# Attention: some of VectorE's subtractions are tied behind others

## The chip, the cores and the metric

The kernel runs on one core of one Trainium2 chip. The number that counts is the time of one execution on the device, in microseconds (us); smaller is better. All matrix products run in float32r, so that a float32 operand is cut into a high part (a rounded copy) and a low part (the operand less its high part), and a product takes three matmuls: high by high, high by low, low by high. The names in the profile follow this: `w_hi`, `w_lo` for weights, `h_hi`, `h_lo` for the normalised input, `wh`, `wl` for the attention weights.

## The reference

One block of a hybrid decoder: attention and an RWKV-7 time mix side by side, then an MLP and gated embeddings. The change lies in the attention and in the projections that run beside it.

```
def stick_breaking_attention(q, k, v):          # (B, S, H, Dh), 8 heads of 64, S = 512
    for blk in range(seq // Q_BLOCK):           # 128 queries each
        z = einsum('bhqd,bhkd->bhqk', q[block], k[:kend]) * scale
        mask = s_pos < t_pos
        log_om = where(mask, log_sigmoid(-z), 0.0)
        rev = cumsum(log_om, reverse=True)
        log_w = log_sigmoid(z) + rev - log_om
        w = where(mask, exp(log_w), 0.0)
        outs.append(einsum('bhqk,bhkd->bhqd', w, v[:kend]))

def reference(x, ...):
    h = rms_norm(x, attn_norm_g)
    u = h @ w_in                                # 1024 x 5376: q, k, v, time mix, gates
    o_sb = stick_breaking_attention(q, k, v)
    o_rw = rwkv7_time_mix(u_rw, ...)
    merged = g_sb * (o_sb @ w_up_sb) + g_rw * (o_rw @ w_up_rw)
    x = x + merged @ w_out
    ...                                         # MLP, embeddings, final norm
```

## The kernel before

**Weights.** Weights come in units of 128x1024 float32. `fetch_to` makes a unit ready: a DMA fills `w_raw`, ScalarE (ACT) casts it to `w_hi` (L225), and VectorE (DVE) subtracts to get `w_lo` (L227, 128x1024). It runs ahead of use: while one unit is multiplied, two further ones are fetched, and there are three buffers of `w_hi` and `w_lo`. In the attention stage the units are q, k and v of each pair of heads and then the first units of the time mix.

**Projections.** A projection of q, k or v is 8 steps of `mm3` (L244, L245, L246: three matmuls of 128x512 into `ps_m`, or `ps_z` for two of the early ones). `projected` then takes the result out of PSUM on DVE (L447 for q, L459 for k, L467 for v). For q it makes the high halves on ACT and GpSimd (POOL) and the low halves `ql` on DVE (L455, two of 64x512); for k the high halves `kk` on ACT (L462) and the low ones on DVE (L463, two of 64x512); v is turned by PE and split (L477, L478).

**Attention.** There are eight heads, in four pairs. `scores` makes three blocks of z in PSUM for a head (L511 with high q, L512 with low q, L513 for the mask), softplus of it on ACT (L516, L517, L518) and DVE (L519), and splits that into `sph` (ACT, L274) and `spl` (DVE, L275). Partial sums of it go through DVE (L528, L531) and POOL (L527, L532, L533). `attend` adds the running sums with PE (L558 and L562, from `sph`, `spl` and the sums), takes the exponential on ACT (L563), makes `wh` (L564) and `wl` (L565) on DVE, and multiplies them with v on PE (L550); L571 and L572 take the output out of PSUM.

**Order.** `drive` interleaves the steps of a head's `attend`, of the next head's `scores`, and 11 steps of the projections ahead. Each engine runs its own queue in order. The order within a queue is made when the program is built, by a scheduler that goes by dependencies and its own estimates of time; `tc.issue_after(x)` adds one more condition, that what is written inside it stands behind x in the queue of the same engine. `state["lo"]` is the last DVE subtraction of `split`, which is the helper for `sph` and `spl`.

Of the kernel before, what the change touches and what calls it, by code (L numbers as in the profile page):

```python
# [14 lines left out]
ALU = mybir.AluOpType  # L15
# [25 lines left out]
U_PLE, U_QKV, U_RW, U_GSB, U_GRW, U_UPSB, U_UPRW, U_OUT, U_FF1, U_FF2, U_GATE = range(11)  # L41
# [52 lines left out]
def tile_block(ctx: ExitStack, tc: tile.TileContext, xT, xt, pT, wts, lora, cols_d, gfin_d, consts_d, out, dbg=None):  # L94
    nc = tc.nc
    act, dve, pool, pe, sync = nc.scalar, nc.vector, nc.gpsimd, nc.tensor, nc.sync
# [3 lines left out]
    def r32(ap):  # L100
        return ap.bitcast(F32)
# [34 lines left out]
    seq = []  # L136
# [24 lines left out]
    state = {"i": 0, "used": 0, "due": 0}  # L161
    AHEAD = 3
    homes = {}
# [32 lines left out]
    def made(i):  # L196
# [10 lines left out]
            return sums12.pop(seq[i][1:])[:, 2]  # L207
        return loaded[i]

    def fetch_to(n, ahead=0):  # L210
        while state["i"] < min(n, len(seq)):
            i = state["i"]
            state["i"] += 1
            load_to(i + 1 + ahead)
            raw = made(i)
            if seq[i] in homes:
                hi, lo = homes[seq[i]]()
            elif seq[i][0] == U_S4:
                hi = wpool.tile([P, 512], F32R, name="w_hi4", bufs=1)
                lo = wpool.tile([P, 512], F32R, name="w_lo4", bufs=1)  # L220
            else:
                hi = wpool.tile([P, 1024], F32R, name="w_hi")
                lo = wpool.tile([P, 1024], F32R, name="w_lo")
            with tc.issue_after(state["hx"] if seq[i] == (U_FF1, 4) else state["fourth"][0]) if seq[i] in ((U_FF1, 4), (U_OUT, 2), (U_OUT, 3)) else nullcontext():
                state["cast"] = act.copy(out=hi, in_=raw).ins  # L225
            with tc.issue_after(state["fourth"][1]) if seq[i] in homes and seq[i][0] == U_OUT else nullcontext():
                state["wlo"] = dve.tensor_tensor(out=lo, in0=raw, in1=r32(hi), op=ALU.subtract).ins  # L227
            if seq[i] == (U_OUT, "s", 4):
                state["fourth"] = state["cast"], state["wlo"]
            ready.setdefault(seq[i], []).append((hi, lo))  # L230
# [42 lines left out]
    def split(hi, lo, src):  # L273
        act.copy(out=hi, in_=src)  # L274
        state["lo"] = dve.tensor_tensor(out=lo, in0=src, in1=r32(hi), op=ALU.subtract).ins  # L275
# [54 lines left out]
    with ExitStack() as sA:  # L330
# [43 lines left out]
        with ExitStack() as s1:  # L374
# [68 lines left out]
            def projected(hp, i, ps):  # L443

                if i == 0:
                    t = p1.tile([P, T], F32, name="qT", tag="qkv", bufs=3)
                    dve.scalar_tensor_tensor(out=t, in0=ps, scalar=0.125, in1=rs, op0=ALU.mult, op1=ALU.mult)  # L447

                    qq = [p1.tile([P, T], F32R, name=f"qq{hh}") for hh in range(2)]

                    ql = qls[hp % 2]
                    for hh, (sl, ot) in enumerate((HALVES, HALVES[::-1])):
                        act.copy(out=qq[hh][sl], in_=t[sl])
                        pool.tensor_copy(out=qq[hh][ot], in_=t[sl])
                        dve.tensor_tensor(out=ql[hh][sl], in0=t[sl], in1=r32(qq[hh][sl]), op=ALU.subtract)  # L455
                    heads[hp] = [qq, ql]
                elif i == 1:
                    t = p1.tile([P, T], F32, name="kT", tag="qkv", bufs=3)
                    dve.tensor_tensor(out=t, in0=ps, in1=rs, op=ALU.mult)  # L459
                    kk = [p1.tile([P, T], F32R, name=f"kk{hh}") for hh in range(2)]  # L460
                    for hh, (sl, ot) in enumerate((HALVES, HALVES[::-1])):
                        act.copy(out=kk[hh][sl], in_=t[sl])  # L462
                        dve.tensor_tensor(out=kk[hh][ot], in0=t[sl], in1=r32(kk[hh][sl]), op=ALU.subtract)  # L463
                    heads[hp].append(kk)
                else:
                    t = p1.tile([P, T], F32, name="vT", tag="qkv", bufs=3)
                    dve.tensor_tensor(out=t, in0=ps, in1=rs, op=ALU.mult)  # L467
                    late.append([3, hp, t])
# [29 lines left out]
            def scores(hp, hh, got):  # L498

                qq, ql, kk = heads[hp][:3]  # L500
                sp = p1.tile([P, 1280], F32, name="sp")
                sph = p1.tile([P, 1280], F32R, name="sph")
                spl = p1.tile([P, 1280], F32R, name="spl")
                zt = {}
                got.update(zt=zt, sp=sp, sph=sph, spl=spl)
                for b, js in BLOCKS:
                    zt[b] = ps_z()

                    for j in js:
                        s = slice(j * P, (j + 1) * P)  # L510
                        pe.matmul(z(zt, j), kk[hh][:, s], qq[hh][:, j * P:T], start=j < 3, stop=False, skip_group_check=True)  # L511
                        pe.matmul(z(zt, j), kk[hh][:, s], ql[hh][:, j * P:T], start=False, stop=False, skip_group_check=True)  # L512
                        pe.matmul(z(zt, j, 0, P), ident_b, caus_b, start=False, stop=True, skip_group_check=True)  # L513
                    s, n = BANKS[b]
                    e = sp[:, s:s + n]
                    act.activation(out=e, in_=zt[b][:, :n], func=AF.Abs)  # L516
                    act.activation(out=e, in_=e, func=AF.Exp, scale=-1.0)  # L517
                    act.activation(out=e, in_=e, func=AF.Ln, bias=1.0)  # L518
                    dve.scalar_tensor_tensor(out=e, in0=zt[b][:, :n], scalar=0.0, in1=e, op0=ALU.max, op1=ALU.add)  # L519
                    split(sph[:, s:s + n], spl[:, s:s + n], e)  # L520
                    if b == 1:

                        sums = p1.tile([P, 512], F32, name="sums", bufs=1)
                        hi, lo = (p1.tile([P, 640], F32R, name=name) for name in ("sums_hi", "sums_lo"))
                        for to, i in ((0, 2), (256, 1)):
                            for part, d in ((sph, hi), (spl, lo)):
                                pool.tensor_copy(out=d[:, to:to + P], in_=part[:, ZB[i]:ZB[i] + P])  # L527
                        dve.tensor_tensor(out=sums[:, 0:P], in0=sp[:, ZB[2] + P:ZB[2] + 2 * P], in1=sp[:, ZB[3]:ZB[3] + P], op=ALU.add)  # L528
                        split(hi[:, P:2 * P], lo[:, P:2 * P], sums[:, 0:P])
                        for c, other in ((0, sp[:, ZB[2]:ZB[2] + P]), (P, sums[:, 0:P])):  # L530
                            dve.tensor_tensor(out=sums[:, 256 + c:384 + c], in0=sp[:, ZB[1] + P + c:ZB[1] + 2 * P + c], in1=other, op=ALU.add)  # L531
                        pool.tensor_copy(out=hi[:, 384:640], in_=sums[:, 256:512])  # L532
                        pool.tensor_tensor(out=lo[:, 384:640], in0=sums[:, 256:512], in1=r32(hi[:, 384:640]), op=ALU.subtract)  # L533
                        got["later"] = hi, lo
                    yield

            def attend(hp, hh, got):

                vv, oo = heads[hp][3:]
                sl = HALVES[hh]  # L540
                zt, sp, sph, spl = (got[n] for n in ("zt", "sp", "sph", "spl"))
                wh = p1.tile([P, 1280], F32R, name="wh")
                wl = p1.tile([P, 1280], F32R, name="wl")
# [11 lines left out]
                for b, js in BLOCKS:  # L555
                    s, n = BANKS[b]
                    for part in (sph, spl):
                        pe.matmul(zt[b][:, :n], tri, part[:, s:s + n], start=False, stop=False, skip_group_check=True)  # L558
                    j = js[0]
                    for part, later in zip((sph, spl), got["later"]):  # L560
                        after = (later[:, 256:640], later[:, 0:256], part[:, ZB[3]:ZB[3] + P])[j]
                        pe.matmul(z(zt, j, P), neg, after, start=False, stop=part is spl, skip_group_check=True)  # L562
                    state["exp"] = act.activation(out=sp[:, s:s + n], in_=zt[b][:, :n], func=AF.Exp)  # L563
                    dve.tensor_copy(out=wh[:, s:s + n], in_=sp[:, s:s + n])  # L564
                    dve.tensor_tensor(out=wl[:, s:s + n], in0=sp[:, s:s + n], in1=r32(wh[:, s:s + n]), op=ALU.subtract)  # L565
                    yield
                    output(before)
                    before = js
# [68 lines left out]
        with ExitStack() as s2:  # L637
# [37 lines left out]
            for hp in range(HP):  # L675
                csl = slice(hp * P, (hp + 1) * P)
                for i, (name, got) in enumerate((("w0", cum_), ("a0", a_all))):
# [3 lines left out]
                    t = p2.tile([P, T], F32, name=name, bufs=HP)  # L681
# [929 lines left out]
    with tc.issue_after(s_):  # L1611
        act.preload_act_table_set(LNEXP)

        r, n = (r4[:, i, tt:tt + 1] for i in (1, 2))
# [74 lines left out]
```

## Time and profile before

| | us |
|---|---|
| median of 3 runs | 856.06 (855.99 to 856.78) |
| the profiled execution | 859.3 |
| its span, first to last instruction | 857.5 |
| DVE busy over the span | 712.6 (83%) |
| ACT busy over the span | 513.1 (60%) |
| POOL busy over the span | 105.5 (12%) |

The attention stage lies between about 20 and 140 us of the span. The granted TensorE clock is 0.996 of full speed in the mean. Matmuls overlap in the profile, so that their starts, not their durations, tell where TensorE (PE) lost time: in an undisturbed row of 128x512 matmuls one starts every 0.23 us, though each is shown as 0.39 us long.

### The profile page before, as it was taken

The numbers are of one execution on the slowest core, as the hardware profiler recorded it, in microseconds if no ns is written. First come the engines' busy times: TensorE is split into PE (matmuls) and PEld (weight loads), VectorE is DVE, ScalarE is ACT, GpSimd is POOL, SyncE is SP. The second block draws the span as 40 slices with busy tenths as digits, with TensorE's granted clock in tenths as the row PEclk, the third lists the DMA queues.
The fourth block names the chain that finished last, engine by engine and source line by source line (L and its number), as shares of the span: only waits on it lengthen the run. The fifth ranks groups of instructions, "written<-read, shape, count | busy, mean of one in ns | idle before, by whom it ended". The sixth has DMA issues, their size and how long they took to land.

```text
span 857.5 us, 14647 instructions
## 1 busy us (share of the span) xinstructions
PE 840.8 (98%) x5594; PEld 697.5 (81%) x5594; DVE 712.6 (83%) x1264; ACT 513.1 (60%) x804; POOL 105.5 (12%) x174
## 2 busy tenths in 40 slices
PE   8999999999999999999999999999999999999996
PEld 5778788777777777777888888899889989988885
DVE  7989987896987969867896597899879988997767
ACT  7878887734436243533585575458647844783843
POOL 1332432001212101020000101000110010010000
PEclk9999999999999999999999999999999999999999
DMA  8311213421220323427882676973985489275402
GB/s 320 101 50 62 87 62 135 123 96 54 63 88 25 103 83 115 162 97 232 284 258 95 189 228 156 232 202 102 227 234 150 139 240 241 96 221 145 174 23 99
DMA packets 40197, 124.23 MB, mean 145 GB/s; under 512 B 4544, under 2 KB 4544, under 8 KB 40128
## 3 DMA queue, kind: packets, MB, share of 16 engines
q1 hardware_dynamic: 34944, 104.42, 35.7%
q0 software_dynamic: 5184, 18.88, 12.1%
q8 instruction: 44, 0.72, 0.4%
q14 instruction: 25, 0.20, 0.1%
HBM read 108.08 MB, written 10.49 MB: 138 GB/s over the span
## 4 chain that ended last, share of the span: by engine, by line
PE 87%; DVE 9%; issue 1%; ACT 1%; DMA 1%; SPq 0%; DVEq 0%; ACTq 0%
PE ps_m L244 14%; PE ps_m L245 14%; PE ps_m L246 14%; PE ps_m L260 9%; PE ps_m L259 9%; PE ps_m L261 9%; PE ps_g L877 1%; DVE w_lo L227 1%; PE ps_o L550 1%; PE ps_s L1005 1%; PE ps_z L558 1%; PE ps_c L996 1%; PE ps_g L967 1%; DVE LX L899 1%; DVE own L888 1%
## 5 line engine op out<-in xcount | busy, mean ns | idle before, releaser
L225 ACT CAST w_hi<-w_raw 128x1024 fp32r<-128x1024 f32 x122 | 128.0, 1051 | 122.4 <-PE ps_m L245 77.4
L227 DVE TENSOR_TENSOR w_lo<-w_raw,w_hi 128x1024 fp32r<-128x1024 f32 x122 | 149.0, 1224 | 24.2 <-ACT w_hi L225 23.5
L244 PE MATMUL ps_m<-h_hi,w_hi 128*128 128x512 f32 x320 | 130.6, 410 | 0.8 <-ACT w_hi L274 0.7
L246 PE MATMUL ps_m<-h_hi,w_lo 128*128 128x512 f32 x320 | 128.6, 402 | 0.0
L245 PE MATMUL ps_m<-h_lo,w_hi 128*128 128x512 f32 x320 | 128.2, 401 | 0.3 <-DVE h_lo L407 0.3
L244 PEld LDWEIGHTS ps_m<-h_hi,w_hi 128*128 128x128 f32 x320 | 60.7, 190 | 12.6 <-ACT w_hi L274 1.1
L246 PEld LDWEIGHTS ps_m<-h_hi,w_lo 128*128 128x128 f32 x320 | 60.4, 189 | 12.0
L245 PEld LDWEIGHTS ps_m<-h_lo,w_hi 128*128 128x128 f32 x320 | 60.5, 189 | 11.3 <-DVE h_lo L407 1.3
L245 PE MATMUL ps_m<-hx,w_hi 128*128 128x256 f32 (+1 forms) x208 | 65.8, 316 | 0.0
L244 PE MATMUL ps_m<-hx,w_hi 128*128 128x256 f32 (+1 forms) x208 | 65.8, 316 | 0.0
L246 PE MATMUL ps_m<-hx,w_lo 128*128 128x256 f32 (+1 forms) x208 | 65.7, 316 | 0.0
L244 PE MATMUL ps_m<-tb,w_hi 128*128 128x256 f32 x192 | 54.3, 283 | 0.0
L245 PE MATMUL ps_m<-tb,w_hi 128*128 128x256 f32 x192 | 54.3, 283 | 0.0
L246 PE MATMUL ps_m<-tb,w_lo 128*128 128x256 f32 x192 | 54.3, 283 | 0.0
L259 PE MATMUL ps_m<-w_hi,fS 128*128 128x512 f32 x128 | 49.8, 389 | 0.0
L260 PE MATMUL ps_m<-w_lo,fS 128*128 128x512 f32 x128 | 49.8, 389 | 0.0
L261 PE MATMUL ps_m<-w_hi,fS 128*128 128x512 f32 x128 | 49.8, 389 | 0.0
L245 PEld LDWEIGHTS ps_m<-hx,w_hi 128*128 128x128 f32 x208 | 39.6, 191 | 3.0 <-DVE hx L1158 0.4
L244 PEld LDWEIGHTS ps_m<-hx,w_hi 128*128 128x128 f32 x208 | 39.6, 191 | 2.8 <-ACT hx L1157 0.2
L246 PEld LDWEIGHTS ps_m<-hx,w_lo 128*128 128x128 f32 x208 | 39.6, 191 | 2.5
L259 PE MATMUL ps_m<-w_hi,fA 128*128 128x512 f32 x96 | 37.4, 389 | 0.0
L260 PE MATMUL ps_m<-w_lo,fA 128*128 128x512 f32 x96 | 37.4, 389 | 0.0
(425 smaller groups left out, 2147.2 us busy)
## 6 DMA issues: line engine op xcount, KB each, us to landing
w_raw<-in_wts_dram SPq DMA_DIRECT2D x129, 512.0 KB, 4.0
gates<-gg SPq DMA_DIRECT2D x16, 256.0 KB, 2.0
w_raw<-in_wts_dram POOLq DMA_DIRECT2D x8, 512.0 KB, 6.6
x_in<-in_xT_dram SPq DMA_DIRECT2D x8, 256.0 KB, 5.5
gb<-gates SPq DMA_DIRECT2D x8, 256.0 KB, 4.5
tmp<-gates SPq DMA_DIRECT2D x8, 256.0 KB, 2.9
upsb<-tmp SPq DMA_DIRECT2D x8, 256.0 KB, 5.1
ga<-upsb SPq DMA_DIRECT2D x8, 256.0 KB, 6.2
```

The costliest lines, as they stand in the source:

```text
L225: state["cast"] = act.copy(out=hi, in_=raw).ins
L227: state["wlo"] = dve.tensor_tensor(out=lo, in0=raw, in1=r32(hi), op=ALU.subtract).ins
L244: pe.matmul(ps, wh, xh[:, k, t], start=first, stop=False, skip_group_check=skip)
L245: pe.matmul(ps, wh, xl[:, k, t], start=False, stop=False, skip_group_check=skip)
L246: pe.matmul(ps, wl, xh[:, k, t], start=False, stop=last, skip_group_check=skip)
L259: pe.matmul(ps, xh[:, k + j], wh, start=first and j == 0, stop=False, skip_group_check=True)
L260: pe.matmul(ps, xh[:, k + j], wl, start=False, stop=False, skip_group_check=True)
L261: state["row"] = pe.matmul(ps, xl[:, k + j], wh, start=False, stop=last and j == 1, skip_group_check=True).ins
L550: pe.matmul(ps_o[:, j * P:T], vv[:, j, hh, :, :].rearrange("p a d -> p (a d)"), part[:, ZB[j]:ZB[j] + ZN[j]], start=j == 2 and part is wh, ...
L558: pe.matmul(zt[b][:, :n], tri, part[:, s:s + n], start=False, stop=False, skip_group_check=True)
L877: last = pe.matmul(ps[rows, k], left[rows, k, :], rhs[rows, k], start=True, stop=True)
L888: dve.tensor_tensor(out=own8[rows], in0=own, in1=b8[rows].broadcast_to([32, 8, 32]), op=ALU.mult)
```

## The change

`state["urgent"]` remembers the DVE subtraction that PE will ask for soonest: the last `spl` of a block of scores, or the last `wl` of a block of attention weights. Three other subtractions are tied behind the one that is current when they are written: `w_lo` of the units of q, k, v and of the time mix, `ql`, and the low halves of `kk`. No instruction is added, removed or changed in size.

```
+    def behind():
+        return tc.issue_after(state["urgent"]) if "urgent" in state else nullcontext()
...
-            with tc.issue_after(state["fourth"][1]) if seq[i] in homes and seq[i][0] == U_OUT else nullcontext():
+            with tc.issue_after(state["fourth"][1]) if seq[i] in homes and seq[i][0] == U_OUT else behind() if seq[i][0] in (U_QKV, U_RW) else nullcontext():
                 state["wlo"] = dve.tensor_tensor(out=lo, in0=raw, in1=r32(hi), op=ALU.subtract).ins
...
-                        dve.tensor_tensor(out=ql[hh][sl], in0=t[sl], in1=r32(qq[hh][sl]), op=ALU.subtract)
+                        with behind():
+                            dve.tensor_tensor(out=ql[hh][sl], in0=t[sl], in1=r32(qq[hh][sl]), op=ALU.subtract)
...
-                        dve.tensor_tensor(out=kk[hh][ot], in0=t[sl], in1=r32(kk[hh][sl]), op=ALU.subtract)
+                        with behind():
+                            dve.tensor_tensor(out=kk[hh][ot], in0=t[sl], in1=r32(kk[hh][sl]), op=ALU.subtract)
...
                     split(sph[:, s:s + n], spl[:, s:s + n], e)
+                    state["urgent"] = state["lo"]
...
-                    dve.tensor_tensor(out=wl[:, s:s + n], in0=sp[:, s:s + n], in1=r32(wh[:, s:s + n]), op=ALU.subtract)
+                    state["urgent"] = dve.tensor_tensor(out=wl[:, s:s + n], in0=sp[:, s:s + n], in1=r32(wh[:, s:s + n]), op=ALU.subtract).ins
```

The scheduler answers with another order in the attention stage: DVE's queue changes from the first head on to the last, PE's and ACT's in a few places, and one store on the DMA queue trades places with a load. Behind that stage the queues are as before. The places below are those that the prediction speaks of. A number behind a name tells buffers apart; the line numbers of the changed kernel lie 3 to 6 higher.

DVE before, while the queries of the last pair of heads (`qT_1008`) are made and the fifth head's attention weights (`wh_998`, `wl_999`) are due:

```order
L519 SCALAR_TENSOR_TENSOR sp_875<-ps_z_974,sp_875 128x512
L447 SCALAR_TENSOR_TENSOR qT_1008<-ps_m_903,rs_87 128x512
L227 TENSOR_TENSOR w_lo_1051<-w_raw_949,w_hi_1050 128x1024
L275 TENSOR_TENSOR spl_877<-sp_875,sph_876 128x512
L564 CAST wh_998<-sp_875 128x256
L455 TENSOR_TENSOR ql10_196<-qT_1008,qq0_1010 64x512
L565 TENSOR_TENSOR wl_999<-sp_875,wh_998 128x256
```

and DVE at the same place in the changed kernel:

```order
L524 SCALAR_TENSOR_TENSOR sp_875<-ps_z_974,sp_875 128x512
L450 SCALAR_TENSOR_TENSOR qT_1008<-ps_m_903,rs_87 128x512
L278 TENSOR_TENSOR spl_877<-sp_875,sph_876 128x512
L570 CAST wh_998<-sp_875 128x256
L571 TENSOR_TENSOR wl_999<-sp_875,wh_998 128x256
L459 TENSOR_TENSOR ql10_196<-qT_1008,qq0_1010 64x512
L459 TENSOR_TENSOR ql11_197<-qT_1008,qq1_1011 64x512
```

`w_lo_1051` has gone from ahead of `spl_877` to a place seven instructions behind the `wl_999` shown here, and `ql10` now stands behind `wl_999`.

DVE before, about 10 us later, when the keys of the last pair (`kT_1119`) are ready:

```order
L459 TENSOR_TENSOR kT_1119<-ps_m_1018,rs_87 128x512
L227 TENSOR_TENSOR w_lo_1144<-w_raw_1048,w_hi_1143 128x1024
L463 TENSOR_TENSOR kk0_1121<-kT_1119,kk0_1121 64x512
L463 TENSOR_TENSOR kk1_1122<-kT_1119,kk1_1122 64x512
L519 SCALAR_TENSOR_TENSOR sp_1022<-ps_z_1109,sp_1022 128x512
```

and in the changed kernel:

```order
L463 TENSOR_TENSOR kT_1119<-ps_m_1018,rs_87 128x512
L524 SCALAR_TENSOR_TENSOR sp_1022<-ps_z_1109,sp_1022 128x512
L578 TENSOR_TENSOR oo_966<-ps_o_1000,oo_966 64x512
L570 CAST wh_1147<-sp_1022 128x256
L278 TENSOR_TENSOR spl_1024<-sp_1022,sph_1023 128x512
L468 TENSOR_TENSOR kk0_1121<-kT_1119,kk0_1121 64x512
L468 TENSOR_TENSOR kk1_1122<-kT_1119,kk1_1122 64x512
L230 TENSOR_TENSOR w_lo_1144<-w_raw_1048,w_hi_1143 128x1024
L571 TENSOR_TENSOR wl_1148<-sp_1022,wh_1147 128x256
```

The low halves of the keys now stand behind four instructions of the head that is under way, and `wl_1148` behind both halves and a `w_lo`.

PE in the changed kernel, where the scores of the last pair's first head (`ps_z_1163`) begin, from keys `kk0_1121`:

```order
L564 MATMUL ps_z_1066<-sph_1023,tri_190 128x512
L564 MATMUL ps_z_1066<-spl_1024,tri_190 128x512
L568 MATMUL ps_z_1066<-sums_hi_1080,neg_191 128x256
L568 MATMUL ps_z_1066<-sums_lo_1081,neg_191 128x256
L247 MATMUL ps_m_1127<-h_hi_85,w_hi_951 128x512
L248 MATMUL ps_m_1127<-h_lo_86,w_hi_951 128x512
L249 MATMUL ps_m_1127<-h_hi_85,w_lo_952 128x512
L516 MATMUL ps_z_1163<-qq0_1010,kk0_1121 128x256
```

Before, `ps_z_1163` stood ahead of these rows and of one more step of three matmuls: PE asks for `kk0_1121` ten matmuls later than it did.

## The prediction

> **What bounds the kernel now.** I read the page first (busy times, then the chain that ended last), then busy times by 20 us (in the row: PE, PEld, DVE, ACT, POOL, each with its count), then PE's waits in the attention stage (total, times, longest), and last the timeline at each place where PE lost time.
>
> ```profile
> PE 840.8 (98%) x5594; PEld 697.5 (81%) x5594; DVE 712.6 (83%) x1264; ACT 513.1 (60%) x804; POOL 105.5 (12%) x174
> ...
> PE 87%; DVE 9%; issue 1%; ACT 1%; DMA 1%; SPq 0%; DVEq 0%; ACTq 0%
> ...
> 80.00:100.00 20.00, 19.16 (x100) 15.56 (x100) 18.80 (x33) 16.38 (x32) 7.24 (x10) 1.00 0.20 66
> ...
> PE ps_o L550 <- DVE wl L565: 0.8, 2, 0.5
> ```
>
> PE is busy 98% of the span and has 87% of the chain, so only what makes PE lose time counts. The change touches the attention stage. There DVE is nearly as full as PE: 18.80 of 20 us against 19.16, with ACT at 16.38. Where PE waits there, it waits for the subtractions and casts that DVE makes for it: 0.8 us in two places for `wl`, and less for `spl` and `wh`. The profile ends a matmul later than PE can start the next, so I count lost time by starts: the distance to the next start less the usual one, which is 0.23 us behind 512 columns (0.22 between the last two rows quoted for the sixth head below) and half of that behind 256. By that rule the stops quoted below come to 0.58, 0.21, 0.45, 0.81 and 0.20, 2.25 us in all. No DVE work is removed. The change can win only by taking a `w_lo`, `ql` or `kk` out of the way at these places, and it pays wherever the work put off comes in the way of something else, or where DVE, with that work tied back, has nothing to do.
>
> **The change part by part.** I go through the places in order of time; "late" means PE against the same instruction before.
>
> First head, around 48 us.
>
> ```profile
> 48.21 0.50 PE L550 MATMUL ps_o<-wh,vv 128*128 128x512 f32 x1
> 49.02 0.51 PE L550 MATMUL ps_o<-wl,vv 128*128 128x512 f32 x1 [0.30 <-DVE wl L565]
> ...
> 45.15 1.40 DVE L463 TENSOR_TENSOR kk<-kT,kk 64x512 fp32r<-64x512 f32 x2
> 47.13 0.69 DVE L519 SCALAR_TENSOR_TENSOR sp<-ps_z,sp 128x512 f32<-128x512 f32 x1 [0.58 <-ACT sp L518]
> ...
> 48.27 0.69 DVE L565 TENSOR_TENSOR wl<-sp,wh 128x512 fp32r<-128x512 f32 x1
> ...
> 46.47 0.63 ACT L518 ACTIVATE sp<-sp 128x512 f32<-128x512 f32 x1
> ```
>
> PE asks for `wl` at 48.44 and starts at 49.02: 0.58 lost. Ahead of that `wl` stands the `sp` at 47.13, for which DVE sat idle 0.58 us until ACT was done with L518. So the `w_lo` and the two `kk` ahead of it cost nothing here, though they filled DVE. In the changed queue both `kk` and that `w_lo` stand behind the `spl` that follows; DVE then idles longer, and L518, `sp`, `wh` and `wl` come when they came. The stops of this head before it do not matter either, since PE meets ACT's chain here again. **Term: 0.** Below: 0.58 is won if the whole chain of ACT moves forward; above: 0.4, half of one `spl` and one `wh` queued ahead.
>
> Second head's exponentials, around 55 us. Here the work put off has to be done.
>
> ```profile
> 43.91 1.21 DVE L227 TENSOR_TENSOR w_lo<-w_raw,w_hi 128x1024 fp32r<-128x1024 f32 x1
> ...
> 50.08 0.28 DVE L531 TENSOR_TENSOR sums<-sp,sums 128x128 f32<-128x128 f32 x1
> ...
> 55.14 0.28 PE L550 MATMUL ps_o<-wl,vv 128*128 128x256 f32 x1
> ```
>
> Before, DVE was through with the sums at 50.36 and went on to `oo`, `sp`, `spl`, `wh`. Now the `kk` pair (1.40) and `w_lo` (1.21) come first, 2.4 us with the usual overlap of some 0.1 between neighbours, so the `sp` begins near 52.8. Behind it stand `oo`, `wh`, `spl` (0.6, 0.2, and `spl` only when ACT's `sph`, 0.62, is there), and `wl` ends near 55.1, against 55.14 on PE. So nothing is lost if all goes well; 0.7 is lost if POOL's work on the sums slows a `kk` by 0.5 (the next rows) and the rest of the way slips by 0.2. **Term: +0.3,** near the middle, because there is no margin.
>
> ```profile
> 77.05 1.19 DVE L463 TENSOR_TENSOR kk<-kT,kk 64x512 fp32r<-64x512 f32 x1
> ...
> 76.96 0.73 POOL L533 TENSOR_TENSOR sums_lo<-sums,sums_hi 128x256 fp32r<-128x256 f32 x1
> ```
>
> The longer `kk` is what I mean: 1.19 us beside POOL's 0.73, where the pair above took 1.40 together; 0.5 more. The changed order puts `kk` right behind the sums, where POOL works. The Trainium skill speaks against the change here: SBUF — State Buffer, section "SBUF: two separate sides", has it that a GpSimd instruction that reads SBUF holds the port pair it shares with VectorE for its whole length, and a VectorE instruction with two SBUF inputs then waits fully. By that rule a `kk` waits up to the whole 0.73, where the row shows 0.5; the sum would be up to 0.2 higher by it. The term goes by the row.
>
> Third head, around 68 us.
>
> ```profile
> 64.11 0.63 ACT L518 ACTIVATE sp<-sp 128x512 f32<-128x512 f32 x1
> 64.65 1.25 ACT L453 CAST qq<-qT 64x512 fp32r<-64x512 f32 x2
> ...
> 66.33 0.62 ACT L274 CAST sph<-sp 128x512 fp32r<-128x512 f32 x1
> ...
> 65.56 1.38 DVE L455 TENSOR_TENSOR ql<-qT,qq 64x512 fp32r<-64x512 f32 x2
> 66.98 0.69 DVE L275 TENSOR_TENSOR spl<-sp,sph 128x512 fp32r<-128x512 f32 x1
> 67.59 0.29 DVE L564 CAST wh<-sp 128x256 fp32r<-128x256 f32 x1
> ...
> 68.07 0.31 PE L550 MATMUL ps_o<-wh,vv 128*128 128x256 f32 x1
> 68.39 0.39 PE L550 MATMUL ps_o<-wl,vv 128*128 128x256 f32 x1
> ```
>
> Before, both `ql` ran ahead of `spl`, while ACT was still at `sph`. Now `spl` comes first, then both `ql`, then `wh`. ACT reaches the end of `sph` no sooner than L518, the two casts and `sph` allow: 64.11 + 0.63 + 1.25 + 0.62 = 66.6. Add `spl` 0.69 and `ql` 1.38: `wh` begins at 68.65 and ends at 68.95, where PE wants it at 68.07 + 0.3. That is 0.6 lost. The `w_lo` of this stretch now stands ahead of `wh` and `wl` of the head before, which can make all this up to 0.8 later. I take 0.75. In return, PE asks for `wl` three matmuls later, and its 0.21 goes. **Term: +0.54** (bounds -0.21 and +1.2).
>
> Fifth head, around 94 us, the first pair of queues shown under the change.
>
> ```profile
> 91.57 1.22 DVE L227 TENSOR_TENSOR w_lo<-w_raw,w_hi 128x1024 fp32r<-128x1024 f32 x1
> 92.70 1.10 DVE L275 TENSOR_TENSOR spl<-sp,sph 128x512 fp32r<-128x512 f32 x1
> 93.72 0.70 DVE L564 CAST wh<-sp 128x256 fp32r<-128x256 f32 x1
> ...
> 91.74 0.38 ACT L563 ACTIVATE sp<-ps_z 128x256 f32<-128x256 f32 x1
> ...
> 93.80 0.39 PE L246 MATMUL ps_m<-h_hi,w_lo 128*128 128x512 f32 x1
> 94.48 0.39 PE L550 MATMUL ps_o<-wh,vv 128*128 128x256 f32 x1 [0.30 <-DVE wh L564]
> 95.41 0.38 PE L550 MATMUL ps_o<-wl,vv 128*128 128x256 f32 x1 [0.54 <-DVE wl L565]
> ```
>
> `w_lo` (1.22) goes from ahead of `spl`, `ql` (0.67) from ahead of `wl`. ACT's exponential is done at 92.13, so `wh` and `wl` can be over near 93.5; PE asks at 94.03 and 94.15. Both stops go: 94.48 - 94.03 = 0.45 and 95.41 - 94.60 = 0.81. **Term: -1.26.** The margin of 0.6 makes this the surest term.
>
> Sixth head, around 107 us, with the keys of the last pair (the second place shown under the change).
>
> ```profile
> 103.95 1.41 DVE L463 TENSOR_TENSOR kk<-kT,kk 64x512 fp32r<-64x512 f32 x2
> 105.39 0.69 DVE L519 SCALAR_TENSOR_TENSOR sp<-ps_z,sp 128x512 f32<-128x512 f32 x1
> ...
> 104.21 0.63 ACT L518 ACTIVATE sp<-sp 128x512 f32<-128x512 f32 x1
> ...
> 105.48 0.39 ACT L563 ACTIVATE sp<-ps_z 128x256 f32<-128x256 f32 x1
> ...
> 104.84 0.31 PE L511 MATMUL ps_z<-qq,kk 128*128 128x256 f32 x1
> 105.15 0.48 PE L244 MATMUL ps_m<-h_hi,w_hi 128*128 128x512 f32 x1
> ...
> 107.33 0.39 PE L244 MATMUL ps_m<-h_hi,w_hi 128*128 128x512 f32 x1
> 107.55 0.39 PE L245 MATMUL ps_m<-h_lo,w_hi 128*128 128x512 f32 x1
> ```
>
> Before, the `kk` pair ended at 105.36 and the scores that read it had begun at 104.84, on its first half. PE now asks ten matmuls later: at 107.33 less the 0.31 that the scores take, 107.0; with the terms so far (-0.42), 106.6. But the first `kk` now waits for `spl`: ACT's L518 ends at 104.84; `sp` 0.69 to 105.55; ACT is free behind the exponential at 105.87; `sph` 0.62, `spl` 0.69, `kk` 0.70: 107.85. **Term: +1.27.** Bounds: +0.6 if the earlier win takes ACT's chain forward by 0.7 (a good half of the `w_lo` of 1.22), +1.8 if DVE brings lag along. `wl` behind the `kk` pair and `w_lo` is ready at 110.0, when PE, which asks for it five matmuls later than before, gets there.
>
> Last head, around 133 us.
>
> ```profile
> 133.03 0.39 PE L246 MATMUL ps_m<-h_hi,w_lo 128*128 128x512 f32 x1
> 133.46 0.35 PE L550 MATMUL ps_o<-wh,vv 128*128 128x256 f32 x1
> ```
>
> 0.20 is lost to `wh`; a `w_lo` leaves its front. **Term: -0.20.** The later `w_lo` are not missed: units are fetched two ahead of use, more than 10 us. Behind 140 us the queues are the old ones, and PE's lag is handed through.
>
> The sum is 0 + 0.3 + 0.54 - 1.26 + 1.27 - 0.20 = +0.65 us. It is made against the profiled execution, 859.3 us with a span of 857.5; the median of the runs is 3.2 lower, and I carry the difference over: 856.06 + 0.65 = **856.7**. With every bound low it would be -0.58 - 0.21 - 1.26 + 0.6 - 0.20 = -1.65, with every one high 0.4 + 0.7 + 1.2 - 1.26 + 1.8 - 0.2 = +2.64.
>
> **The rivals.** *The put-off work finds gaps.* If DVE gains so much room that neither `ql` nor `kk` is ever late, and ACT's chains move forward with it, the whole 2.25 goes: **853.8**. For it: the winning term has a margin, and the scheduler moved the scores back by ten matmuls to suit. Against it: DVE's 18.80 of 20 leaves 1.2 us per 20, and a queue in order spends them waiting at its head.
>
> *DVE's lag is handed on.* Slower than before: with `kk`, `ql` and `w_lo` tied back, DVE stands idle at `sp` for ACT (0.58 at 47.13 already, about 2 us once `kk` and `w_lo` are gone from there), and the same work then delays the next `sp`, so ACT's next chain, so the next. It decides from the point where one such idle stretch is longer than what DVE makes up before the next key or query: with 1.2 us free per 20, idling of 2 us is not made up in a head. The high ends then come together: +2.6, **858.7**. Against it: the `w_lo` are freely movable and can fall into later idle time.
>
> *It does not do what it says* is out: the queues show the new order. That it is all absorbed, 856.1, lies in my forecast's range.
>
> **How the numbers follow.** Forecast (gain and loss of like size, 854.4 to 857.7): 0.5. Gaps found: 0.2. Lag handed on: 0.3. A measurement can tell about 0.2%, 1.7 us: faster means below 854.35, slower above 857.77. So 0.2, 0.5 and 0.3. The range goes past the low bound (854.4) most of the way to the first rival, and to the second rival's price: 854.0 to 858.7.
>
> **What would show it.** Right: no stop at 94 us; ahead of the scores of the last pair's first head, PE idle about 1 us for DVE's `kk`; DVE idle about 2 us near 45 us; a stop on `wh` near 68. Wrong: if those scores start without idle time, the fifth term falls and the first rival gains; if PE still stops near 94, the gain falls; if PE stops grow from head to head and DVE's idle time with them, it is the second.

## The result and the profile after

| | before | after |
|---|---|---|
| median of 5 runs each, us | 856.06 (855.30 to 856.78) | 859.47 (858.16 to 860.72) |
| ratio of the times, 95% interval | | 1.0043 (1.0032 to 1.0055) |
| profiled execution, us | 859.3 | 859.37 |

The changed kernel is slower by 2.7 to 4.7 us. The prediction was 856.7 with a range to 858.7, so it missed, on the side of its second rival.

Three executions among the runs below that were clearly longer (915, 1077 and 4691 us) are left out of the ratios; of the two that were profiled, the one with `kk` and `ql` tied ran at a granted clock of 0.85 all through the attention stage, so that its stretches are not given, while the other kept a clock of 1.00 up to 700 us, so that its attention stage can be read.

The two profiles have the same span, 857.5 us, and so cannot be compared as wholes. The profiled execution of before was 3.2 us over its own median, and the busy times by stretches show one place, far behind the change, with a lower granted clock (the last figure but two of a row) than in the changed kernel. Before, then after:

```profile
300.00:400.00 100.00, 97.00 (x1025) 74.88 (x1024) 78.51 (x194) 41.74 (x68) 12.15 (x26) 0.98 0.40 131
```

```profile
300.00:400.00 100.00, 98.37 (x1097) 75.66 (x1096) 80.94 (x199) 43.56 (x71) 12.18 (x26) 1.00 0.43 136
```

What can be compared is the attention stage by itself. A group of four transposes (of the values, `vT`) stands in it once for each pair of heads. The last stretch is closed by the first matmul on `h_hi` behind the first six on `lx` and `lxl`. The distances of these starts measure how long each stretch took, whatever happened ahead of it. The timeline of before gives 28.25, 57.55, 84.89, 114.46 and 150.01; the first and last rows of the four in the changed kernel:

```profile
28.27 0.60 PE L479 MATMUL ps_m<-cst,vT 128*128 128x128 f32 x4
...
117.39 0.60 PE L479 MATMUL ps_m<-cst,vT 128*128 128x128 f32 x4
```

with 58.37 and 86.62 between them and 152.64 for the matmul that closes the last stretch. The four stretches take 29.30, 27.34, 29.57 and 35.55 us before and 30.10, 28.25, 30.77 and 35.25 after: +0.80, +0.91, +1.20 and -0.30, together +2.61 of the +3.4. Every stretch with a key or query in it became longer. The other 0.8 lies within the uncertainty of the time. Behind the last stretch the profile of the changed kernel has 704.9 us left (857.5 - 152.64), and the ten profiles of the runs below that are not among those three executions have 703.6 to 706.4, so nothing there sets the changed kernel apart.

PE's waits from 20 to 140 us in the changed kernel (total, times, longest) say for what:

```profile
PE ps_z L516 <- DVE kk L468: 2.3, 1, 2.3
PE ps_o L556 <- DVE wh L570: 0.9, 1, 0.9
PE ps_o L556 <- DVE wl L571: 0.9, 2, 0.6
```

The waits for `wl` and `wh` that before showed at 94 us are gone, as forecast. In their place stand one for `wl` behind the matmul at 54.96, one for `wh` behind that at 68.67, and one for `kk` behind that at 107.06, which is the largest (its rows stand under the run with `kk` alone). PE at the first two:

```profile
54.96 0.36 PE L556 MATMUL ps_o<-wh,vv 128*128 128x256 f32 x1
55.87 0.39 PE L556 MATMUL ps_o<-wl,vv 128*128 128x256 f32 x1 [0.55 <-DVE wl L571]
...
68.67 0.39 PE L249 MATMUL ps_m<-h_hi,w_lo 128*128 128x512 f32 x1
70.00 0.39 PE L556 MATMUL ps_o<-wh,vv 128*128 128x256 f32 x1 [0.94 <-DVE wh L570]
```

Counted by starts the three lose 0.79, 1.10 and 2.41 us. The reverse side is DVE's waits for ACT, from 20 to 120 us, before and after:

```profile
DVE sp L519 <- ACT sp L518: 1.4, 3, 0.6
```

```profile
DVE sp L524 <- ACT sp L523: 4.9, 4, 2.5
```

DVE now stands idle 4.9 us ahead of `sp` where it stood 1.4, and has the same work to do. That is what the second rival said would be seen. The timeline of the changed kernel shows the two long ones, near 47 and 107 us, with what follows:

```profile
47.06 0.69 DVE L524 SCALAR_TENSOR_TENSOR sp<-ps_z,sp 128x512 f32<-128x512 f32 x1 [1.92 <-ACT sp L523]
...
50.31 1.49 DVE L468 TENSOR_TENSOR kk<-kT,kk 64x512 fp32r<-64x512 f32 x2
51.84 1.65 DVE L230 TENSOR_TENSOR w_lo<-w_raw,w_hi 128x1024 fp32r<-128x1024 f32 x1
...
55.41 0.41 DVE L571 TENSOR_TENSOR wl<-sp,wh 128x256 fp32r<-128x256 f32 x1
...
103.42 0.68 DVE L463 TENSOR_TENSOR kT<-ps_m,rs 128x512 f32<-128x512 f32 x1
106.62 0.69 DVE L524 SCALAR_TENSOR_TENSOR sp<-ps_z,sp 128x512 f32<-128x512 f32 x1 [2.52 <-ACT sp L523]
...
108.87 1.40 DVE L468 TENSOR_TENSOR kk<-kT,kk 64x512 fp32r<-64x512 f32 x2
```

At 47 us DVE idles 1.92, and from 50.31 on it does `kk` and `w_lo` one behind the other, 3.1 us, in front of the `wl` that PE wants at 55. At 104.1 it is through with `kT`. Before, it went straight on to a `w_lo` and both `kk`; now it idles 2.52 first.

### The profile page after: what moved, and what is told of

The parts are those of the page before. It is cut to its first block, busy times and chain, and to the rows that moved or that the text cites. A ratio compares the mean times of both kernels' runs of the same rounds, so it can differ in the third digit from the quotient of the medians.

```text
span 857.5 us, 14642 instructions
## 1 busy us (share of the span) xinstructions
PE 839.4 (98%) x5594; PEld 696.4 (81%) x5594; DVE 712.7 (83%) x1264; ACT 512.8 (60%) x804; POOL 108.7 (13%) x174
## 4 chain that ended last, share of the span: by engine, by line
PE 46%; DVE 2%; ACT 1%; issue 1%; ACTq 0%; DVEq 0%
PE ps_m L262 9%; PE ps_m L263 9%; PE ps_m L264 9%; PE ps_m L248 6%; PE ps_m L249 6%; PE ps_m L247 6%; PE ps_m L1159 1%; ACT w_hi L228 0%; DVE ga L1218 0%; ACT aside L1117 0%; DVE hx L278 0%; DVE hx L1164 0%; DVE mg L278 0%; DVE xs L1541 0%; DVE t L1540 0%
```

## The experiments

Theory A says that the time is lost where DVE idles for ACT and hands its lag on. Theory B says that the order on `kk` merely costs its own wait. Theory C puts the loss behind the attention stage. After the first four runs (`kk` left free, `kk` alone, `w_lo` alone, and the last pair's `ql` with one `w_lo`) A was made sharper as theory D: from 84 to 107 us DVE's queue is the bound, so that only idling in it, or work that leaves it for a gap behind, changes the time. The expectations name D's rivals E, F and G where they stand. The table gives, for each, the ratio to before in the same comparison, the change of the median, and the four stretches (before: 29.30, 27.34, 29.57, 35.55). The line numbers differ by a few from run to run.

| tied | ratio (95%) | us | stretches |
|---|---|---|---|
| `w_lo` | 0.9996 (0.9987 to 1.0005) | -0.25 | 29.27, 27.22, 29.93, 35.25 |
| `ql` | 1.0004 (0.9995 to 1.0013) | +0.62 | 29.28, 27.03, 29.92, 35.55 |
| `kk` | 1.0009 (1.0000 to 1.0018) | +0.71 | 29.27, 27.46, 30.24, 35.56 |
| `w_lo`, `ql` | 1.0010 (0.9998 to 1.0021) | +1.20 | 29.31, 28.00, 30.00, 35.26 |
| `kk`, `ql` | 1.0014 (1.0005 to 1.0023) | +1.30 | not given |
| `kk`, `w_lo` | 1.0033 (1.0020 to 1.0046) | +2.34 | 30.14, 27.46, 31.02, 35.25 |
| all (the change) | 1.0043 (1.0032 to 1.0055) | +3.41 | 30.10, 28.25, 30.77, 35.25 |
| all but the last pair's `kk` | 1.0029 (1.0016 to 1.0042) | +2.69 | 30.15, 28.25, 30.23, 35.26 |
| last pair's `ql`, one `w_lo` | 0.9998 (0.9989 to 1.0007) | -0.11 | 29.32, 27.34, 29.75, 35.54 |
| none, one `w_lo` twice | 1.0015 (1.0006 to 1.0024) | +1.10 | 29.30, 27.35, 30.30, 35.54 |
| `w_lo`, the last put off further | 0.9984 (0.9972 to 0.9996) | -1.39 | 29.31, 27.23, 28.83, 35.26 |
| the same, and the last pair's `ql` | 0.9991 (0.9982 to 1.0000) | -0.75 | 29.31, 27.21, 28.85, 35.25 |
| last pair's `ql`, one `w_lo`; next `w_lo` on POOL | 1.0038 (1.0025 to 1.0051) | +3.37 | 29.36, 27.35, 32.63, 35.56 |

**The orders one by one and two by two.** Without the order on `kk`:

```
-                        with behind():
-                            dve.tensor_tensor(out=kk[hh][ot], ...)
+                        dve.tensor_tensor(out=kk[hh][ot], ...)
```

> After without its order on the keys' low halves; w_lo and ql keep theirs. Theory A (a lag handed on): with the keys' halves in front of the softplus's sums again, DVE has work while ACT computes them, so its wait at sp near 106 us (2.52 us in after) and TensorE's wait for kk at 107 (2.41 between starts) both go, the halt at 94 (1.26) stays gone, and the two at 55 and 68 us (0.79 and 1.10) shrink to some extent: 856.06 - 1.26 - 0.20, plus 0 to 1.7 for those two, 854.6 to 856.3. Theory B (the keys' order costs just its own wait): after less that wait, 859.47 - 2.41 = 857.1, with the halts at 55 and 68 unchanged. Theory C (the loss lies behind the attention, where TensorE's stops were not added up): about 859.

Measured: before plus 1.2 (1.0010, -0.2 to +1.8 us). The waits at `sp` and for `kk` near 107 went as A said (0.24 for `kk` is left, at 103.81), but a wait for `wl` of 1.42 between starts came in at 107.49 that A had not foreseen. The stop at 55 went too, and 0.85 stayed at 68. It is B's time with A's waits: neither had it whole. C falls, since its 859 lies above the interval.

With the order on `kk` alone, the `behind()` taken from `w_lo` and `ql` instead:

> Before with the order on the keys' low halves alone. Theory A: TensorE waits for kk near 107 us, but for less than in after, since no lag comes from w_lo and ql: its scores are asked for ten matmuls later and spl ends about when it did in before, so 0.6 to 1.8 there by the working for the sixth head; the halts at 94 stay (1.26). 856.06 + 1.2, so 856.7 to 857.9. Theory B: the full 2.41 at 107, plus what stood at 55 and 68, with nothing gained at 94: 858.5 to 860. Theory C: no change, 856.1.

Measured: +0.71. The wait for `kk` is there, with 1.05 between starts (A had 0.6 to 1.8) against 2.41 in the changed kernel. B's 858.5 to 860 falls. The same order costs more than twice as much in the company of the other two, and the timelines say why. With `kk` alone:

```profile
101.82 0.68 DVE L462 TENSOR_TENSOR kT<-ps_m,rs 128x512 f32<-128x512 f32 x1
...
107.27 1.40 DVE L467 TENSOR_TENSOR kk<-kT,kk 64x512 fp32r<-64x512 f32 x2
...
106.82 0.39 PE L249 MATMUL ps_m<-h_hi,w_lo 128*128 128x512 f32 x1
108.10 0.35 PE L515 MATMUL ps_z<-qq,kk 128*128 128x256 f32 x1 [0.89 <-DVE kk L467]
```

and PE in the changed kernel:

```profile
107.06 0.39 PE L249 MATMUL ps_m<-h_hi,w_lo 128*128 128x512 f32 x1
109.70 0.35 PE L516 MATMUL ps_z<-qq,kk 128*128 128x256 f32 x1 [2.26 <-DVE kk L468]
```

From the start of `kT` to that of `kk` it is 107.27 - 101.82 = 5.45 here and 108.87 - 103.42 = 5.45 there. What differs is that DVE reaches `kT` 1.60 later in the changed kernel while PE comes only 0.24 later: 1.05 + 1.60 - 0.24 = 2.41. So the lag that DVE brought along is the whole difference.

With the orders on `w_lo` alone and on `ql` alone:

> Before with the order on w_lo alone. Theory A: w_lo behind wl leaves DVE idle for some tenths at the sums, and the halt at 94 loses only w_lo's part (ql of the last pair still stands in front of wl): 94 gets shorter by 0.4 to 0.8, 55 and 68 get longer by 0 to 0.8 each; 855.3 to 857. No wait for kk at 107. Theory B: 856.06 - 0.6 = 855.5, no halts at 55 and 68 beyond before's. Theory C: no change, 856.1.

> Before with the order on ql alone. Theory D: at 68 us the two ql of the third pair stand in front of wh behind an spl that waits for ScalarE, so a halt of 0.8 to 1.1 there where before has 0.21; at 94 only ql's part goes and w_lo stays in front of wh (0.45 stays, 0.81 shrinks to 0.2 or 0.4), to be handed on to kk at 104 to 107: before plus 0.4 to 1.0, about 856.4. Rival (w_lo's order is what makes spl late at 68): no more at 68 than before has, before plus 0.

Measured: -0.25 and +0.62, both within what can be told from before. With `w_lo`, the 94 us stop shrinks to 0.28, and 1.26 appear at 106.65, for `wl`, behind a `w_lo` that now stands in front of it. DVE is not full all the way there: the `w_lo` that before filled its queue ahead of `kk` is put off, and it idles 0.69 and 0.49 at the two `kk` (102.45 and 103.62) until ACT has cast their high halves. What was put off past that idle time came back at 107. With `ql`, the 94 us stops are 0.68 and 0.34 (before 0.45 and 0.81), and 0.53 for `kk` came at 104.29, handed on as expected. But my expectation failed at 68 us: there is no stop at all. The timeline of that run shows that the order had not been fixed as I took it to be:

```profile
66.55 0.29 DVE L569 CAST wh<-sp 128x256 fp32r<-128x256 f32 x1 [0.68 <-ACT sp L568]
66.88 0.43 DVE L570 TENSOR_TENSOR wl<-sp,wh 128x256 fp32r<-128x256 f32 x1
67.22 0.68 DVE L278 TENSOR_TENSOR spl<-sp,sph 128x512 fp32r<-128x512 f32 x1
67.83 1.38 DVE L459 TENSOR_TENSOR ql<-qT,qq 64x512 fp32r<-64x512 f32 x2
```

With `ql` alone tied, the scheduler also put `wh` and `wl` ahead of `spl`, so PE got them in time. With `w_lo` tied too, `spl` and both `ql` stand ahead of `wh`, and the stop is there (0.85 in the run without the order on `kk`).

Two by two:

> After without its order on w_lo; kk and ql keep theirs. Theory D, in which a halt comes where two put-off pieces meet in front of what TensorE asks for: no halt at 55 (kk stands there alone, 1.5 us, without the 1.65 of w_lo) nor at 68 (ql alone); near 107 a wait for kk of about 1, as with kk ordered alone. Lengths between the four groups of transposes of the values: 29.3, 27.0 to 27.3 and 29.9 to 30.3 (before: 29.30, 27.34, 29.57), so before plus 0.3 to 1.0, about 856.2. Rival G (each order costs what it costs, and the costs add up): kk alone 0.7 and ql alone 0.6, before plus 1.3.

> After without its order on ql; kk and w_lo keep theirs. Theory D: the halt of 0.8 at 55 comes back, since kk and w_lo meet there; at 68 there is none, as no ql stands behind the put-off w_lo; near 107 a wait for kk of 2.2 to 2.6, as w_lo (two of them behind wl and spl) brings the lag. Lengths 30.1, 27.2 to 27.4, 30.6 to 31.0, so before plus 1.6 to 2.4, about 857.6. Rival G: kk 0.7 and w_lo -0.25, before plus 0.45, 856.0.

`kk` with `ql`: +1.30 (+0.4 to +2.0 by the interval), which fits G, and D only near its end; this run tells nothing apart. `kk` with `w_lo`: +2.34 (+1.7 to +3.9), where G's +0.45 is excluded. The stop at 54.64 is back with 0.81, as D said, and 68 us has 0.34; the wait for `kk` is 1.83, less than D's 2.2, and 0.72 came back at 94, which D had not. The lag accounts for that wait too. From the start of `kT` to that of `kk` it is 5.45 a third time (102.61 to 108.06); against `kk` alone DVE reaches `kT` 0.79 later and PE asks 0.01 later, and 1.05 + 0.79 - 0.01 = 1.83. The lag is here the size of the second head's stop, 0.81, and in the changed kernel, with the third head's stop added, twice that.

By the ratios, the single orders sum to +0.0009. The pair `kk` and `w_lo` adds 0.0028 to its two, the pair `w_lo` and `ql` 0.0010, the pair `kk` and `ql` 0.0001: 0.0048 in all, close to the 0.0043 of the change, though each of these ratios is only known to about 0.001. The scheduler makes each run's queues anew, so these sums compare whole kernels and not the price of one order by itself.

**The last pair's keys alone.**

```
-                        with behind():
+                        with behind() if hp < 3 else nullcontext():
                             dve.tensor_tensor(out=kk[hh][ot], ...)
```

> After with the last pair's kk alone left without an order. Theory D: the halts at 55 and 68 us stay (0.8 and 0.9 to 1.1), the wait for kk at 107 (2.41) is replaced by one for wl of 1.2 to 1.5 as in the run without any order on kk, so between the transposes of the third and the last pair's values TensorE loses 0.4 instead of 1.2 against before: after less 0.8, which is before plus 2.2 to 2.8, about 858.2. Theory B (the kk order costs its own wait): after less 2.4, before plus 1.0, 856.7.

Measured: +2.69, and 858.31 where D had 858.2. The stops at 55.19 and 68.91 are 0.79 and 1.09 as in the changed kernel; the one for `kk` is 0.45, and 1.42 for `wl` came at 109.10. Theory B's 856.7 is below the interval.

**Is DVE full from 84 to 107 us?** First, only the last pair's `ql` and the one `w_lo` that stood in front of `wh` at 94 us are tied:

```
+ ... else behind() if seq[i] == (U_RW, 12) else nullcontext():
...
+                        with behind() if hp == 3 else nullcontext():
+                            dve.tensor_tensor(out=ql[hh][sl], ...)
```

> Before with nothing ordered but the last pair's ql and the one w_lo that stand in front of wh and wl at 94 us; DVE's rows differ at this one place. Theory A and B alike: the halt of 1.26 at 94 goes and nothing else moves, 854.8 (854.6 to 855.2), if what is put off there finds a gap before 107; if instead DVE, busy throughout from 84 to 103 us, hands the 1.2 us on, a halt of about that size stands at the next thing that TensorE asks for and the time is 856.0. Theory C: 856.1.

Measured: -0.11. The 94 us stop is gone, the forecast's surest term, and nothing was won, since PE then waits for `kk`, which came no sooner:

```profile
104.13 1.40 DVE L467 TENSOR_TENSOR kk<-kT,kk 64x512 fp32r<-64x512 f32 x2
...
103.23 0.40 PE L249 MATMUL ps_m<-h_hi,w_lo 128*128 128x512 f32 x1
104.97 0.36 PE L515 MATMUL ps_z<-qq,kk 128*128 128x256 f32 x1 [1.34 <-DVE kk L467]
```

Before, `kk` stood at 103.95. A stop of 1.26 became one of 1.51. This is the run from which theory D comes. Its test from the other side adds work, the one `w_lo` computed a second time:

```
                 state["wlo"] = dve.tensor_tensor(out=lo, in0=raw, ...).ins
+                if seq[i] == (U_RW, 12):
+                    dve.tensor_tensor(out=lo, in0=raw, in1=r32(hi), op=ALU.subtract)
```

> Before with the one w_lo of 91.57 us computed a second time on VectorE, which its queue takes up at about 97 us, behind the halts at 94: 1.2 us more of work in the stretch, results as before. Theory D: nothing absorbs it, TensorE waits for kk near 104 us, before plus 0.8 to 1.3, about 856.8. Rival (VectorE has slack there): before plus 0 to 0.3.

Measured: +1.10 (+0.5 to +2.1), for 1.2 us of added work; in the trace a wait for `kk` at 104.61 of 0.67 between starts, and the third stretch is longer by 0.73. DVE has at most some tenths to spare there.

Then work is taken out of the stretch. With `w_lo` tied, the unit whose `w_lo` stood at 106.42 in front of `wl` is kept back until that `wl` is written:

```
+            if seq[i] == (U_RW, 13):
+                state["put_off"] = lo, raw, hi
+            else:
...
+                    if "put_off" in state:
+                        lo, raw, hi = state.pop("put_off")
+                        with behind():
+                            state["wlo"] = dve.tensor_tensor(out=lo, in0=raw, in1=r32(hi), ...).ins
```

> The run with w_lo alone ordered, in which the last w_lo before the last pair (the one at 106.42 us) is put off once more, behind wl, which TensorE waited 1.26 us for there. Theory D (from 84 to 107 us VectorE's queue is the bound, so a halt taken away in it is handed on until something leaves the queue for a gap behind): the 1.26 at 107 goes, as VectorE has a gap of 1.13 at 112.78 to take the 1.22 in; before less 1.2 to 1.5, about 854.4. Rival E (the halt is handed on again, to the next sp or wh that TensorE asks for): as w_lo alone, before less 0.25, 855.5.

Measured: 854.23, -1.39 (0.9984, interval 0.9972 to 0.9996), as D had it and not E. The stop at 106.65 is gone, and the third stretch is 1.10 shorter than with `w_lo` alone tied. The timeline shows where the 1.22 us went: behind `wl`, and out of the 1.13 that DVE idled at the next `sp` in the run with `w_lo` alone (at 112.78), 0.49 are left.

```profile
106.29 0.42 DVE L572 TENSOR_TENSOR wl<-sp,wh 128x256 fp32r<-128x256 f32 x1
106.62 1.22 DVE L576 TENSOR_TENSOR w_lo<-w_raw,w_hi 128x1024 fp32r<-128x1024 f32 x1
...
111.82 0.69 DVE L525 SCALAR_TENSOR_TENSOR sp<-ps_z,sp 128x512 f32<-128x512 f32 x1 [0.49 <-ACT sp L524]
```

This version is faster than both kernels, by 0.3 to 2.4 us against before. The last pair's `ql` tied as well:

> The run with w_lo ordered and the last one put off behind wl, with the last pair's ql behind wl as well, which still stands 0.67 us long in front of wl there at 92.59. Theory D: the 0.30 between starts at 93.52 goes, and up to 0.3 of it may come back at kk or at wl near 107: before less 1.2 to 1.7, 854.0, hardly to be told from the run without it. Rival E (handed on in full): as that run, before less 1.4.

Measured: 854.74, -0.75 (0.9991, 0.9982 to 1.0000), which cannot be told from the run without the order on `ql`. In the trace the stop at 93.52 is gone, and 0.21 for `kk` at 103.14 and 0.27 for `wl` at 106.79, where it was 0.13, stand in its place; the third stretch is 28.85 against 28.83. It was handed on in full, which is E's case and lies at the edge of D's "up to 0.3".

**Off DVE altogether.** In the run that ties the last pair's `ql` and one `w_lo`, the next `w_lo` is computed on POOL:

```
+ (pool if seq[i] == (U_RW, 13) else dve).tensor_tensor(out=lo, in0=raw, ...)
```

> The run with only the last pair's ql and one w_lo ordered, in which the next w_lo (1.64 us on VectorE at 102.46, ahead of kk) is computed on GpSimd instead. Theory D: kk comes up to 1.6 us sooner, the wait for it at 103.23 (1.51 between starts) goes, and the 1.26 once taken from 94 us is really gained: before less 1.0 to 1.4, about 854.5. Rival F (two engines in the same memory slow each other): kk and sp beside GpSimd's operation get longer by as much as VectorE was spared, and the time stays at before less 0.1, 855.6.

Measured: 858.99, +3.37 (1.0038, 1.0025 to 1.0051), worse than either had it. Rows of DVE, POOL and PE in its timeline:

```profile
103.23 3.60 DVE L467 TENSOR_TENSOR kk<-kT,kk 64x512 fp32r<-64x512 f32 x2 [0.69 <-ACT kk L466]
...
103.21 2.36 POOL L230 TENSOR_TENSOR w_lo<-w_raw,w_hi 128x1024 fp32r<-128x1024 f32 x1
...
106.26 0.42 PE L515 MATMUL ps_z<-qq,kk 128*128 128x256 f32 x1 [2.64 <-DVE kk L467]
```

and the view of the tile `kk` in that stretch (shortest, middle and longest in ns):

```profile
L467 DVE TENSOR_TENSOR kk<-kT,kk x2: 687/1785/2883, 103.2 to 106.1; 64x512 fp32r<-64x512 f32 x2
```

The first `kk` began 0.02 us after POOL's subtraction and took 2.88 us instead of 0.69: it stood through nearly the whole of POOL's 2.36. Of the 1.64 that DVE was spared, 0.69 went on waiting for ACT's half of `kk`, so that it began only 0.90 sooner (103.23 against 104.13), and then 2.2 were lost. F had the mechanism and too small a price. The section on hardware comes back to it.

## Why the prediction was wrong, point by point

**First head, 0.** Right: PE's stop at 48 us is 0.51 after and was 0.58, and PE is where it was (48.20 against 48.21). DVE's idling, given as about 2 us, is 1.92.

**Second head, +0.3; it was +0.79.** The place and the mechanism were right, two sizes off. I took 1.40 for `kk` and 1.21 for `w_lo`; they took 1.49 and 1.65, both beside POOL's two operations on the sums (0.91 and 1.06 at that place). That is +0.53, on a chain with no margin. I had put POOL's slowing down to a `kk`, and most of it, 0.44, fell on the `w_lo` behind.

**Third head, +0.54; it was 1.10 - 0.21 = +0.89.** The place and the mechanism were right: `spl`, both `ql` and then `wh`, as in the queue that I reckoned with. The size was short: I let PE come 0.3 late, but took ACT's L518 where it stood before, at 64.11. It comes 1.07 later, at 65.18, and PE asks only 0.53 later than I had it (68.90 for 68.37). That is 0.54 more to wait where I had added 0.15. The run with `ql` alone does not test this term, since its queue has `wh` ahead of `spl`; with `ql` left free, 0.34 stays at 68 us. So it takes `ql` and `w_lo` together.

**Fifth head, -1.26, "the surest term".** The stop went, in the changed kernel and wherever that `w_lo` and `ql` moved. But in the run that makes this edit alone the 1.26 came back as 1.51 at `kk`. To count it as a gain of its own was wrong, as the work put off stayed in the same full stretch of DVE's queue.

**Sixth head, +1.27; it was +2.41. This is the step that failed.** As at the third head, I worked it out from where L518 stood before, "ACT's L518 ends at 104.84", and let PE be 0.42 early. But DVE comes to this stretch with the lag of the second and third heads, and hands it to ACT. Before, then after:

```profile
99.37 0.69 DVE L519 SCALAR_TENSOR_TENSOR sp<-ps_z,sp 128x512 f32<-128x512 f32 x1 [0.29 <-ACT sp L518]
...
100.09 0.62 ACT L274 CAST sph<-sp 128x512 fp32r<-128x512 f32 x1 [0.76 <-DVE sp L519]
```

```profile
101.12 0.68 DVE L524 SCALAR_TENSOR_TENSOR sp<-ps_z,sp 128x512 f32<-128x512 f32 x1
...
101.84 0.62 ACT L277 CAST sph<-sp 128x512 fp32r<-128x512 f32 x1 [1.24 <-DVE sp L524]
```

The same `sp` is 1.75 later in the changed kernel, and ACT waits for it. From that `sph` on ACT works without a pause, so the row that I counted from, 104.21 before, comes at 105.96, again 1.75 later. PE's lag, 86.62 - 84.89 = 1.73, was taken back by the 1.26 at 94 us to about 0.4 (104.05 against 103.68 at the first matmul on `sph` behind it), since PE has nothing to wait for there; DVE, full from 84 to 104, could not take it back. With 1.75 more on `kk` and PE asking 0.69 later than the 106.6 I gave (107.06 + 0.23), the term is 1.27 + 1.75 - 0.69 = 2.33, against 2.41 measured. I named this lag as an upper end of +1.8, which was itself too low, and gave the rival that goes by it 0.3, for the reason that `w_lo` would fall into later idle time. The runs with `kk` alone (1.05 there) and with `kk` and `w_lo` (1.83) show the lag to be the difference. Of the 2.0 us by which my sum is short of the stage's loss, this term has 1.1, the second head 0.5 and the third 0.35.

**Last head, -0.20.** Right, a little small: the last stretch is 0.30 shorter wherever `w_lo` is tied as in the change.

By places the changed kernel has 0 + 0.79 + 0.89 - 1.26 + 2.41 - 0.20 = +2.63, and its stretches say +2.61. The second rival, worked out at +2.6, gave the stage's loss and is the right story, though the median lies 0.8 above its 858.7. That its sum agrees is partly luck: it has 0.4 at the first head, where nothing was lost, and 1.2 at the third, 0.3 too much, against 0.6 too little at the sixth. The signs that I named for the forecast (no stop at 94, PE idle for `kk`, DVE idle about 2 us near 45, a stop on `wh` near 68) all came as well, with only the wait for `kk` too long (2.3 us for about 1), so they hardly tell it from this rival; the growth of the stops, 0.79, 1.10, 2.41, does. The rival's story fails in one point, that idling tells by itself. With `kk` alone tied, DVE idles 2.01 us at 47 and nothing is lost at 55. It takes a second piece put off to the same place, as in the run with `kk` and `w_lo` (0.81 there).

## What to carry to other kernels

When a reordering removes a wait on an engine that is full over the whole stretch, ask where in that stretch, or behind it, the work put off finds idle time; without such a gap the wait turns up at the next thing asked for. A lag has to be carried through the sum for each engine by itself: the one that waits may catch up where the one it waits for cannot. Orders that are harmless singly can be costly together, as they pile the work put off in one place, so they are best tried one by one and in pairs.

## What the runs showed of the hardware

A DVE subtraction with two inputs in SBUF, begun 0.02 us after a POOL subtraction of 128x1024, took 2.88 us where it takes 0.69 alone. The Trainium skill says so of the pair of ports that the two share (SBUF — State Buffer, section "SBUF: two separate sides": an exclusive lock for the whole instruction). This run agrees, 2.2 us of standing against POOL's 2.36. The row by which the prediction went, 1.19 us beside a POOL operation of 0.73, shows the same wait: that `kk` ended 0.55 us behind POOL's operation (77.05 + 1.19 against 76.96 + 0.73), and here it is 0.54 (103.23 + 2.88 against 103.21 + 2.36).

After PE had been idle for 2.64 us in that run, its granted clock (the last figure but two) fell for the next 3.6 us or so; after 2.26 us of idling in the changed kernel it did not. Busy times from 106 to 112 us in the run with POOL's `w_lo`:

```profile
106.00:108.00 2.00, 1.74 (x6) 1.48 (x7) 1.94 (x4) 0.45 (x2) 0.00 (x0) 0.60 0.56 207
108.00:110.00 2.00, 2.00 (x7) 1.66 (x7) 1.71 (x5) 1.59 (x5) 0.00 (x0) 0.55 0.18 64
110.00:112.00 2.00, 2.00 (x12) 1.69 (x11) 1.50 (x3) 0.63 (x2) 0.97 (x2) 1.00 0.00 0
```

Matmuls of 512 columns then start every 0.43 us instead of 0.23. The third stretch of that run is 32.63 us, 2.88 longer than without POOL: 1.30 of it is the longer wait for `kk` (2.81 against 1.51 between starts), and most of the rest the clock. The Trainium skill describes such a gate (TensorE: Matmul & The Clock Gate, section "Part 1: The HAM clock gate"), closing after an idle window of about 3.4 us. Here the clock fell behind 2.64 us, and the measurement decides.

The length of the stop is not all that counts. Half the clock shows in the middle of two other profiles too, behind shorter stops among small matmuls: in before's behind 1.37 us, which is the place between 300 and 400 us shown with the result, and in that of the run with all but the last pair's `kk` tied behind 1.25 us, both for some 3 us. In before's:

```profile
306.92 0.38 PE L937 MATMUL ps_g<-LX,LM 32*32 32x32 f32 x12 [1.37 <-issue]
```

```profile
310.00:312.00 2.00, 2.00 (x30) 1.78 (x27) 0.38 (x1) 0.83 (x2) 0.00 (x0) 0.50 0.00 0
```

So no least length follows from these runs, and what else decides stays open. A stop can cost more than itself: in the run with POOL's `w_lo` an estimated 2.88 - 1.30 = 1.6 us behind a wait of 2.8, by one execution.
